# GpSimd's order in the differential attention written out, its casts and joins regrouped, and the retention's first scores one step later

## The chip, the cores and the metric

The kernel runs on one core of a Trainium2 chip. The metric is the device time of one execution in microseconds (us). The engines are TensorE (PE in the profile), VectorE (DVE), ScalarE (ACT), GpSimd (POOL) and SyncE (SP); SP only issues DMAs. GpSimd issues DMAs too, and those stand in its own instruction stream among its arithmetic.

## The reference, cut to what matters

The program is one layer of a diffusion backbone on 1024 tokens of width 1024, with 256 context tokens, batch 1, in float32. One input projection feeds two groups of four heads each: a two-way chunked retention, and a differential attention over 1280 keys. Their outputs side by side go through one output projection; a gated residual and a gated MLP with a convolution of width 3 follow.

```python
# retention, one chunk
scores = jnp.einsum('bhid,bhjd->bhij', qc, kc) * intra
o = (jnp.einsum('bhij,bhje->bhie', scores, vc)
     + jnp.einsum('bhid,bhde->bhie', qc * q_dec[..., None], S))
S = S * c_dec[:, None, None] + jnp.einsum('bhjd,bhje->bhde', kc * k_dec[..., None], vc)

# differential attention: q (B,H,2,Lq,d), k (B,H,2,Lk,d), v (B,H,Lk,dv)
s = jnp.einsum('bhmqd,bhmkd->bhmqk', qb, k).astype(jnp.float32) * scale
p = jax.nn.softmax(s, axis=-1)
a = p[:, :, 0] - lam * p[:, :, 1]
return jnp.einsum('bhqk,bhke->bhqe', a.astype(v.dtype), v)

# each head's output is scaled by its root mean square, then
out_lat = jnp.concatenate([y_ret_lat, y_diff_lat], axis=-1) @ w_out
x = x + g1 * y_lat
h2 = rms_norm(x, norm2_g[l]) * (1.0 + sc2) + sh2
x = x + g2 * conv_ffn(h2, w_up[l], conv_w[l], conv_b[l], w_down[l])
```

## The kernel before

Float32 operands of the projections are split into a high part and a low part (a cast and a subtraction), and each product is three matmuls, here called a triple. The stages lie one after the other on PE: modulation and projections of keys, values and gates; the projection of the queries, with the retention between its triples; the differential attention; the output projection; the MLP.

**Retention.** The projection calls `tick()` after each triple. `beside(outputs(), 1.35, -16.0)` sets a generator of retention steps beside it: its count starts at the third number and grows by the second at each triple, and each step that falls due is emitted there. The first step holds the first score matmuls, `pc<-st,rk`, whose operand `st` DVE makes by an addition (L466).

**Differential attention.** There are 32 units: four heads (h) by eight tiles of 128 queries (qt). A unit runs through the operations of `OPS` (`scores`, `least`, `exp`, `ratio`, ...). The loop over n is the software pipeline: in turn n, operation `op` is emitted for unit n - int(TAU[op]), in the order of the fractions of `TAU`. Turn n thus holds scores of unit n, `values` (pv, L972) of unit n - 3, and the norm of unit n - 4. For PE, DVE, ACT and SP `in_order` pins the engine's order to the order of emission (`FORCE`). GpSimd is not pinned: a scheduler places its instructions by its own model of time, and `tc.issue_after` only says behind which instruction one may come.

The names that the change touches:

- `ratio` (L951, L952): DVE's reciprocal and product for r; `combine` (L955): DVE's p0 += r * p1 over 1280 columns, from which PE transposes (pt, L960) and ACT copies back (aT, L966).
- `square`: ACT's sum of squares (jka, L981) and GpSimd's small product `e` (L983). `rstd`: DVE's `ssa` (L986), then GpSimd's power -0.5 (L987), called the root here. ACT's norm (L990) waits for the root, PE's `pty` (L995) for the norm, and DVE's low part (L1001) follows.
- `wo_gen`: twelve tiles of 128 x 512 for the output projection, four of the retention's output and eight of weights. GpSimd loads a tile into `woraw` (five buffers), ACT casts it (L1106, L1123), GpSimd subtracts for the low part (L1107, L1124).
- `joined_tokens`: for a head and a half of the queries GpSimd adds high and low part of the attention's output into a `woraw` buffer (L1130) and adds that by DMA onto sums in memory (L1132: t2 and t3, or t4). These sums are operands of the output projection, which multiplies sums and differences of blocks. They are `sgd_152` (t1) to `sgd_155` (t4) in the listings, and the sums of weights `wsd`.
- `load(n + 3)`: GpSimd issues the loads of later units' queries, keys and values (L1018, L1021, L1043).

At the attention's end SP issues the rows of x (L1228), the weight sums (L1100) and the operands `raw` (L1335, from t1, t2, ...) of the output projection. There DVE gates each output (L1351), adds it to x (L1352), and makes the low parts `wolo` (L1107) and `wlo` (L1197).

Of the kernel before, what the change touches and what calls it, by code (L numbers as in the profile page):

```python
# [17 lines left out]
P = 128  # L18
# [8 lines left out]
H = 4  # L27
# [39 lines left out]
FORCE = (mybir.EngineType.PE, mybir.EngineType.DVE, mybir.EngineType.Activation, mybir.EngineType.SP)  # L67


def r32(ap):  # L70
    return ap.bitcast(F32)
# [3 lines left out]
def kernel(  # L75
# [16 lines left out]
    nc = tc.nc  # L92
# [28 lines left out]
    def in_order(start, engines=FORCE):  # L121
        last = {}
        for ins in nc.cur_bb.bb.instructions[start:]:
            if ins.engine not in engines:
                continue
            if ins.engine in last:
                order_only(ins, last[ins.engine])
            last[ins.engine] = ins
# [12 lines left out]
    row_d = [dr.tile([32, 32], F32, name=f"row{i}") for i in range(4)]  # L141
# [7 lines left out]
    yr_d = dr.tile([P, H, 512], F32, name="yrd")  # L149
    sg_d = [dr.tile([P, H, 512], F32, name=f"sgd{i}") for i in range(4)]  # L150
    t1_d, t2_d, t3_d, t4_d = sg_d
    ws_d = [dr.tile([P, 4, 512], F32, name=f"wsd{i}") for i in range(4)]
    A11, A12, A21, A22 = [w_out[i][:, c : c + 4, :] for i in range(2) for c in (0, 4)]
# [7 lines left out]
    with ExitStack() as p1:  # L161
# [207 lines left out]
        def outputs():  # L369
            n_pairs, per_head = H * NT // 2, NT // 2  # L370
            pairs, more = {}, states((2, 3))
            for n in range(-2, n_pairs + 3):
                if n + 2 < n_pairs:
                    pairs[n + 2] = Pair(n + 2)
                if n == -2:
                    continue
                if n + 1 < n_pairs:
                    pairs[n + 1].score()
                forming = per_head <= n < 3 * per_head
                if n == per_head - 1 or forming and n % 2 == 0:  # L380
                    next(more)
                yield
                if 0 <= n < n_pairs:
                    pairs[n].output(0)
                yield
                if forming:
                    next(more)
                yield
                if n == n_pairs + 2:
                    for _ in range(4):  # L390
                        yield
                    pairs[n - 3].turn(newest[0])
                elif n >= 3:
                    pairs[n - 3].turn()
                if 0 <= n < n_pairs:
                    pairs[n].output(1)
                    pairs[n].squares()
                yield
                if 0 <= n - 1 < n_pairs:
                    pairs[n - 1].gate()  # L400
                    for _ in range({1: 2, 2: 2}.get(n, 0)):
                        weight_sum(last_y[0])
                if forming:
                    next(more)
                yield
                yield
# [9 lines left out]
        def beside(g, rate, due=0.0):  # L416
            for _ in side["g"]:
                pass
            side.update(g=g, rate=rate, due=due)
# [127 lines left out]
        with ExitStack() as p0:  # L547
# [151 lines left out]
            for k in range(KD):  # L699
# [28 lines left out]
                n = k + 4  # L728
# [179 lines left out]
        for made_key in keyed[:2]:  # L908
            order_only(made_key.ins, rk_turned.ins)
        wg = stream_block(0)  # L910
        beside(outputs(), 1.35, -16.0)
        transposed(wg, None, rtab, 64, 1.0, 0, by_head)
        rtab = load_rope(1)
        wg = stream_block(4)
# [176 lines left out]

    g1 = wo.tile([P, D], F32, name="g1")

    def out_weights(srcs, sl, eng=nc.sync, low=nc.vector, lag=0, after=(), free=0):
        raws = []
        srcs = [src[:, k, :] for src in srcs for k in range(4)]
        for k in range(len(srcs) + lag):
            if k < len(srcs):
                raw = wo.tile([P, 512], F32, name="woraw", bufs=5)
                wo_loads.append(eng.dma_start(out=raw, in_=srcs[k]))  # L1100
                raws.append(raw)
            yield
            if k >= lag:
                whi = wo.tile([P, 512], F32R, name="wohi", bufs=8)
                wlo = wo.tile([P, 512], F32R, name="wolo", bufs=8)
                wo_casts.append(nc.scalar.copy(whi, raws[k - lag]))  # L1106
                part = low.tensor_tensor(out=wlo, in0=raws[k - lag], in1=r32(whi), op=ALU.subtract)  # L1107
                for ins in after if k - lag >= free else ():
                    order_only(part.ins, ins.ins)
                sl.append((whi, wlo))  # L1110

    wo_first, wo_casts, wo_loads = [], [], []
    wo_gen = out_weights((A11, ws_d[0]), wo_first, nc.gpsimd, nc.gpsimd, 2)

    def first_tokens():
        raws = []
        for h in range(H + 2):
            if h < H:
                raws.append(wo.tile([P, 512], F32, name="woraw", bufs=5))
                nc.gpsimd.dma_start(out=raws[h], in_=yr_d[:, h, :])  # L1120
            yield
            if h > 1:
                nc.scalar.copy(yT[0][1][:, h - 2, :], raws[h - 2])  # L1123
                nc.gpsimd.tensor_tensor(out=yT[1][1][:, h - 2, :], in0=raws[h - 2], in1=r32(yT[0][1][:, h - 2, :]), op=ALU.subtract)  # L1124

    wo_gen = itertools.chain(first_tokens(), wo_gen)

    def joined_tokens(h, half):
        raw = wo.tile([P, 512], F32, name="woraw", bufs=5)
        nc.gpsimd.tensor_tensor(out=raw, in0=r32(yT[0][half][:, H + h, :]), in1=r32(yT[1][half][:, H + h, :]), op=ALU.add)  # L1130
        for to in (t4_d,) if half else (t2_d, t3_d):
            nc.gpsimd.dma_start(out=to[:, h, :], in_=raw, accum_op=ALU.add)  # L1132

    with ExitStack() as p2:
        at = p2.enter_context(tc.tile_pool(name="at", bufs=2, reuse_waits="tile"))
        psa = p2.enter_context(tc.tile_pool(name="psa", bufs=1, space=PSUM, reuse_waits="tile"))

        turns = {}
        start = len(nc.cur_bb.bb.instructions)
        order = sorted(TAU.items(), key=lambda it: it[1] % 1.0)  # L1140
        for n in range(n_units + 8):
            if 2 < n < n_units:
                units[n] = Unit(n)
                vars(units[n]).update(fore[n])
            if n == 9:
                with tc.issue_after(units[n - 5].pool_ins.ins):
                    nc.gpsimd.dma_start(out=g1, in_=row_d[0].rearrange("p c -> (p c)").partition_broadcast(P))
            if n in (6, 9, 15, 17, 21, 28):
                with tc.issue_after(units[n - 5].pool_ins.ins):
                    if n == 6:  # L1150
                        nc.gpsimd.dma_start(out=t1_d[:, H - 1, :], in_=yr_d[:, H - 1, :], accum_op=ALU.add)
                    elif n == 9:
                        nc.gpsimd.dma_start(out=t2_d[:, :, :], in_=t1_d[:, :, :])
                    else:
                        i, j, k = {15: (1, 0, 0), 17: (1, 0, 2), 21: (3, 1, 0), 28: (3, 1, 2)}[n]
                        nc.gpsimd.dma_start(out=ws_d[i][:, k : k + 2, :], in_=ws_d[j][:, k : k + 2, :], accum_op=ALU.add)
            if n in (14, 21, 29):
                nc.sync.dma_start(out=t4_d[:, (14, 21, 29).index(n), :], in_=t2_d[:, (14, 21, 29).index(n), :])
            for half, when in ((0, (12, 18, 26, 33)), (1, (16, 24, 31))):
                if n in when:  # L1160
                    with tc.issue_after(units[min(n - 5, n_units - 1)].pool_ins.ins):
                        joined_tokens(when.index(n), half)
            for op, t in order:
                u = n - int(t)
                if 0 <= u < n_units and (u > 1 or op not in EARLY) and (op, u) not in MOVED:
                    turns[op, u] = len(nc.cur_bb.bb.instructions)
                    units[u].run(op)
                    turns[op, u] = nc.cur_bb.bb.instructions[turns[op, u]]
                for o, v in MOVED.get((op, u), ()):
                    units[v].run(o)  # L1170
                if op == "f" and n >= 9 and n not in (12, 16, 18, 24, 26, 31, 33):
                    with tc.issue_after(units[min(n - 6, n_units - 1)].pool_ins.ins):
                        next(wo_gen, None)
            if n + 3 < n_units:
                after = units[n - 5].pool_ins if n >= 5 else last_va[0]
                with tc.issue_after(after.ins):
                    fore.append(load(n + 3))
        in_order(start)
    aload.close()


# [753 lines left out]
```

## Time and profile before

| what | value |
|---|---|
| median of 3 runs | 1365.8 us (1365.76 to 1365.85) |
| the profiled execution | 1365.33 us, span 1363.5 us, granted clock 0.998 |
| PE | 1348.6 us busy, 99% of the span |
| DVE, ACT, POOL | 998.3, 749.6 and 341.7 us busy |
| attention, 440 to 625.7 us | PE busy 183.6 of 185.7 us, POOL 91.5 |
| chain that ended last | PE 87%, DVE 5%, ACT 3%, issue 2%, DMA 1%, POOL 1% |

Times inside the profile count from the start of the span. A timeline row gives start, duration, engine, source line, operation, output and inputs, the number of instructions that the row joins, and in brackets the engine's idle time before it with what ended it. PE's matmuls are pipelined and their ends modelled: a row's duration may overlap the next row, so PE's progress is read from start to start.

### The profile page before, as it was taken

How to read it: one execution, taken by the hardware profiler on the slowest of the kernel's cores; microseconds unless marked ns; L12 is line 12 of the kernel's file. 1: busy time of each engine (PE TensorE's matmuls, PEld its weight loads, DVE VectorE, ACT ScalarE, POOL GpSimd, SP SyncE). 2: the span in 40 equal slices, each digit the busy share in tenths (PEclk: the TensorE clock that was granted, in tenths of full speed). 3: DMA queues.
4: the chain of work that ended last, by engine and by line, in shares of the span. 5: the costliest groups of instructions: out<-in, count | busy, mean ns of one | idle time of the engine just before them, and what ended most of it. 6: DMA issues, size and time to landing. Idle time of an engine off the chain costs nothing.

```text
span 1363.5 us, 19850 instructions
## 1 busy us (share of the span) xinstructions
PE 1348.6 (99%) x6978; PEld 1134.9 (83%) x6978; DVE 998.3 (73%) x1514; ACT 749.6 (55%) x1429; POOL 341.7 (25%) x433
## 2 busy tenths in 40 slices
PE   9999999999999999999999999999999999999997
PEld 6788888888898899998887788888888888888886
DVE  4746874425775899897989986677776777798856
ACT  4643312424765789997547555445554455455543
POOL 1210004403776436543021222221222110000001
PEclk9999999999999999999999999999999999999999
DMA  9567897655866769855954898988888875963523
GB/s 369 216 255 241 296 314 245 190 181 157 214 174 168 177 153 182 169 109 157 342 166 113 194 233 217 224 218 226 214 213 214 220 193 172 371 214 101 177 93 124
DMA packets 130492, 279.71 MB, mean 205 GB/s; under 512 B 13700, under 2 KB 34948, under 8 KB 129480
## 3 DMA queue, kind: packets, MB, share of 16 engines
q1 hardware_dynamic: 100440, 212.99, 45.8%
q0 software_dynamic: 29376, 64.00, 25.6%
q10 hardware_dynamic: 576, 1.44, 0.3%
q8 instruction: 55, 0.90, 0.3%
q14 instruction: 45, 0.37, 0.1%
HBM read 212.31 MB, written 69.75 MB: 207 GB/s over the span
## 4 chain that ended last, share of the span: by engine, by line
PE 87%; DVE 5%; ACT 3%; issue 2%; DMA 1%; POOL 1%; POOLq 0%; DVEq 0%; ACTq 0%
PE chain L135 6%; PE chain L133 6%; PE chain L134 6%; PE c L134 5%; PE c L133 5%; PE c L135 5%; PE pv L972 4%; PE pl L133 4%; PE pl L135 4%; PE pl L134 4%; PE pA L940 4%; PE pn L135 3%; PE pn L134 3%; PE pn L133 3%; PE third L134 3%; PE third L133 3%
## 5 line engine op out<-in xcount | busy, mean ns | idle before, releaser
L1269 POOL DMA_DIRECT2D cmb<-w_up x80 | 73.9, 1151 | 180.4 <-DMA cmb<-w_up 142.8
L133 PE MATMUL pl<-hT,whi 128*128 128x512 f32 x256 | 105.4, 412 | 0.0
L133 PE MATMUL chain<-T,whi 128*128 128x512 f32 x264 | 102.9, 391 | 0.0
L134 PE MATMUL chain<-T,whi 128*128 128x512 f32 x264 | 102.6, 389 | 0.0
L135 PE MATMUL chain<-T,wlo 128*128 128x512 f32 x264 | 102.4, 390 | 0.2 <-DVE wlo L1197 0.2
L135 PE MATMUL pl<-hT,wlo 128*128 128x512 f32 x256 | 100.1, 391 | 0.0
L134 PE MATMUL pl<-hT,whi 128*128 128x512 f32 x256 | 99.9, 390 | 0.0
L943 DVE TENSOR_REDUCE mt<-pA 128x1 f32<-128x1280 f32 x64 | 95.2, 1489 | 6.1 <-PE pA L940 4.6
L947 ACT ACTIVATE p<-pA,mt 128x1280 f32<-128x1280 f32 x64 | 85.5, 1336 | 9.4 <-DVE mt L943 8.7
L133 PE MATMUL c<-whi,ghl 128*128 128x512 f32 x232 | 90.2, 389 | 0.0
L134 PE MATMUL c<-wlo,ghl 128*128 128x512 f32 x232 | 90.2, 389 | 0.0
L135 PE MATMUL c<-whi,ghl 128*128 128x512 f32 x232 | 90.2, 389 | 0.0
L940 PE MATMUL pA<-ks,qhl 128*128 128x512 f32 (+1 forms) x384 | 89.6, 368 | 0.6 <-ACT p L947 0.5
L1193 ACT CAST whi<-cmb 128x512 fp32r<-128x512 f32 x60 | 37.5, 627 | 85.2 <-PE chain L134 63.0
L940 PEld LDWEIGHTS pA<-ks,qhl 128*128 128x128 f32 x384 | 68.1, 189 | 12.9 <-ACT p L947 1.3
L972 PE MATMUL pv<-va,aT 128*128 128x128 f32 x640 | 77.3, 276 | 0.8 <-DVE yT L1001 0.5
L972 PEld LDWEIGHTS pv<-va,aT 128*128 128x128 f32 x640 | 74.0, 192 | 2.3 <-DVE yT L1001 1.3
L1193 ACT CAST whi<-wra 128x512 fp32r<-128x512 f32 x54 | 33.1, 623 | 68.9 <-PE third L134 40.2
L133 PE MATMUL third<-yT,whi 128*128 128x512 f32 x168 | 65.4, 389 | 0.0
L134 PE MATMUL third<-yT,whi 128*128 128x512 f32 x168 | 65.4, 389 | 0.0
L135 PE MATMUL third<-yT,wlo 128*128 128x512 f32 x168 | 65.4, 389 | 0.0
L133 PE MATMUL pn<-whi,hT 128*128 128x512 f32 x160 | 64.7, 405 | 0.0
(342 smaller groups left out, 3842.2 us busy)
## 6 DMA issues: line engine op xcount, KB each, us to landing
cmb<-w_up POOLq DMA_DIRECT2D x80, 256.0 KB, 6.5
wm<-w_mod SPq DMA_DIRECT2D x32, 512.0 KB, 5.5
cmb<-w_up SPq DMA_DIRECT2D x60, 256.0 KB, 5.2
raw<-w_in SPq DMA_DIRECT2D x27, 512.0 KB, 5.7
wra<-w_up SPq DMA_DIRECT2D x23, 512.0 KB, 6.2
W<-w_down SPq DMA_DIRECT2D x44, 256.0 KB, 6.2
wrb<-w_up SPq DMA_DIRECT2D x40, 256.0 KB, 4.5
ad<-s SPq DMA_DIRECT2D x20, 512.0 KB, 5.7
```

Source lines behind the costliest of these rows:

```text
L133: mm(ps, lh, rh, start=first, stop=False, skip_group_check=more)
L134: mm(ps, lh, rl, start=False, stop=False, skip_group_check=more)
L135: return mm(ps, ll, rh, start=False, stop=last, skip_group_check=more)
L940: mm(self.pa[m][:, c0:c1], self.q[:, m, i, qs], self.k[:, m, c0:c1], start=(i == 0), stop=(i == 1))
L943: nc.vector.tensor_reduce(out=self.mt[:, m : m + 1], in_=self.pa[m][:, :LK], axis=AX.X, op=ALU.min)
L947: nc.scalar.activation(self.p[m], self.pa[m][:, :LK], AF.Exp, scale=-1.0, bias=self.mt[:, m : m + 1], accum_out=self.s[:, m : m + 1])
L972: mm(self.pv, self.aT[:, c, :], self.v[:, c, :], start=(c == 0), stop=(c == NKT - 1))
L1193: cast = nc.scalar.copy(hi, src)
L1269: nc.gpsimd.dma_start(out=o, in_=src, accum_op=ALU.add)
```

## The change

Four things are changed.

1. GpSimd's order in the attention is pinned as the other engines' is (`FORCE` plus `Pool`). In each turn it is: root, then at most one addition (a low part or a join), then DMA issues, then `e`, then the next units' loads. `beside_roots(n)` is called right behind `rstd` and holds all that was spread over three places.
2. A tile of `wo_gen` is loaded in one turn, cast by ACT two turns later, and its low part made by GpSimd one turn after the cast. Before, cast and low part were of one turn. No tile is taken in turns 13 and 21, nor where a join stands.
3. Joins have tiles of their own (`joined`, two buffers, in the pool `at`) and no longer take `woraw` buffers.
4. `beside(outputs(), 1.35, -17.6)`: the count starts 1.6 lower.

The diff, cut to its core:

```diff
-        beside(outputs(), 1.35, -16.0)
+        beside(outputs(), 1.35, -17.6)
...
-    wo_gen = out_weights((A11, ws_d[0]), wo_first, nc.gpsimd, nc.gpsimd, 2)
...
+    def out_ahead():
+        srcs = [yr_d[:, h, :] for h in range(H)] + [w[:, k, :] for w in (A11, ws_d[0]) for k in range(4)]
+        raws, parts = [], []
+        for n in range(len(srcs) + 3):
+            if n > 2:
+                hi, lo = parts[n - 3]
+                nc.gpsimd.tensor_tensor(out=lo, in0=raws[n - 3], in1=r32(hi), op=ALU.subtract)
+            if n < len(srcs):
                 raws.append(wo.tile([P, 512], F32, name="woraw", bufs=5))
-                nc.gpsimd.dma_start(out=raws[h], in_=yr_d[:, h, :])
+                nc.gpsimd.dma_start(out=raws[n], in_=srcs[n])
+            if 1 < n < len(srcs) + 2:
+                i = n - 2
...
+                cast = nc.scalar.copy(parts[i][0], raws[i])
...
             yield
...
     def joined_tokens(h, half):
-        raw = wo.tile([P, 512], F32, name="woraw", bufs=5)
+        raw = at.tile([P, 512], F32, name="joined", bufs=2)
...
+    def beside_roots(n):
+        for half, when in ((0, (12, 18, 26, 33)), (1, (16, 24, 31))):
+            if n in when:
+                joined_tokens(when.index(n), half)
+                break
+        else:
+            if n >= 9 and n not in (13, 21):
+                next(wo_gen, None)
+        if n == 6:
+            nc.gpsimd.dma_start(out=t1_d[:, H - 1, :], in_=yr_d[:, H - 1, :], accum_op=ALU.add)
+        elif n == 8:
+            nc.gpsimd.dma_start(out=g1, in_=row_d[0].rearrange("p c -> (p c)").partition_broadcast(P))
+        elif n == 9:
+            nc.gpsimd.dma_start(out=t2_d[:, :, :], in_=t1_d[:, :, :])
+        elif n in (15, 17, 22, 28):
+            i, j, k = {15: (1, 0, 0), 17: (1, 0, 2), 22: (3, 1, 0), 28: (3, 1, 2)}[n]
+            nc.gpsimd.dma_start(out=ws_d[i][:, k : k + 2, :], in_=ws_d[j][:, k : k + 2, :], accum_op=ALU.add)
...
-            for half, when in ((0, (12, 18, 26, 33)), (1, (16, 24, 31))):
-                if n in when:
-                    with tc.issue_after(units[min(n - 5, n_units - 1)].pool_ins.ins):
-                        joined_tokens(when.index(n), half)
...
-                if op == "f" and n >= 9 and n not in (12, 16, 18, 24, 26, 31, 33):
-                    with tc.issue_after(units[min(n - 6, n_units - 1)].pool_ins.ins):
-                        next(wo_gen, None)
+                if op == "f" and u >= 0:
+                    beside_roots(n)
...
-        in_order(start)
+        in_order(start, FORCE + (mybir.EngineType.Pool,))
```

In the change's file the lines of `wo_gen` and the joins have other numbers (subtraction L1119, load L1122, cast L1130, join L1139 and its DMA L1141, the rest L1152 to L1159), and all from the output projection on stand ten lower (L1228 is L1238 there).

GpSimd in the middle of the attention, from one root (L987) on, before:

```order
L987 TENSOR_TENSOR ssa<-ssa,mhalf 128x1
L1124 TENSOR_TENSOR yT_4484<-woraw,yT_4482 128x512
L1130 TENSOR_TENSOR woraw<-yT_4481,yT_4483 128x512
L983 TENSOR_TENSOR e<-sa 128x1
L1100 DMA woraw<-w_out 128x512
L1132 DMA sgd_153<-woraw 128x512
L1132 DMA sgd_154<-woraw 128x512
L987 TENSOR_TENSOR ssa<-ssa,mhalf 128x1
```

and now:

```order
L987 TENSOR_TENSOR ssa<-ssa,mhalf 128x1
L1139 TENSOR_TENSOR joined<-yT_4481,yT_4483 128x512
L1141 DMA sgd_153<-joined 128x512
L1141 DMA sgd_154<-joined 128x512
L983 TENSOR_TENSOR e<-sa 128x1
L987 TENSOR_TENSOR ssa<-ssa,mhalf 128x1
L1119 TENSOR_TENSOR yT_4484<-woraw,yT_4482 128x512
L1122 DMA woraw<-w_out 128x512
L983 TENSOR_TENSOR e<-sa 128x1
```

Two additions between two roots have become one behind each root, and `e` stands behind the DMA issues.

GpSimd at the attention's end, where the last join of t2 and t3 stands, before:

```order
L987 TENSOR_TENSOR ssa<-ssa,mhalf 128x1
L983 TENSOR_TENSOR e<-sa 128x1
L1130 TENSOR_TENSOR woraw<-yT_4481,yT_4483 128x512
L1132 DMA sgd_153<-woraw 128x512
L1132 DMA sgd_154<-woraw 128x512
L987 TENSOR_TENSOR ssa<-ssa,mhalf 128x1
L983 TENSOR_TENSOR e<-sa 128x1
L987 TENSOR_TENSOR ssa<-ssa,mhalf 128x1 x2
```

and now:

```order
L987 TENSOR_TENSOR ssa<-ssa,mhalf 128x1
L983 TENSOR_TENSOR e<-sa 128x1
L987 TENSOR_TENSOR ssa<-ssa,mhalf 128x1
L1139 TENSOR_TENSOR joined<-yT_4481,yT_4483 128x512
L1141 DMA sgd_153<-joined 128x512
L1141 DMA sgd_154<-joined 128x512
L983 TENSOR_TENSOR e<-sa 128x1
L987 TENSOR_TENSOR ssa<-ssa,mhalf 128x1
L983 TENSOR_TENSOR e<-sa 128x1
L987 TENSOR_TENSOR ssa<-ssa,mhalf 128x1
```

The join and its DMAs stand one root later: three roots followed them, and now two.

SP's queue at the same place (`x_4` to `x_7` are rows of x, `sgd_152` is t1 and `sgd_153` is t2), as a difference:

```order
-L1228 DMA x_7_6792<-x 128x1024
-L1335 DMA raw_6793<-sgd_152 128x2048
-L1100 DMA woraw<-wsd_159 128x512
-L1228 DMA x_4_6789<-x 128x1024
-L1228 DMA x_5_6790<-x 128x1024
-L1228 DMA x_6_6791<-x 128x1024
-L1100 DMA woraw<-wsd_159 128x512 x3
-L1335 DMA raw_6793<-sgd_153 128x2048
```

```order
+L1100 DMA woraw<-wsd_159 128x512 x4
+L1100 DMA woraw<-wsd_157 128x512
+L1238 DMA x_7_6792<-x 128x1024
+L1345 DMA raw_6793<-sgd_152 128x2048
+L1345 DMA raw_6793<-sgd_153 128x2048
+L1238 DMA x_4_6789<-x 128x1024
+L1238 DMA x_5_6790<-x 128x1024
+L1238 DMA x_6_6791<-x 128x1024
```

The weight sums have moved ahead, and the load of t2 now stands ahead of `x_4` to `x_6`.

More of the change, by code (lines that the diff above doesn't have):

```diff
@@ L1092, with out_weights @@
     g1 = wo.tile([P, D], F32, name="g1")
-    def out_weights(srcs, sl, eng=nc.sync, low=nc.vector, lag=0, after=(), free=0):
+    def out_weights(srcs, sl, lag=0, after=(), free=0):
         raws = []
@@ L1099, in out_weights @@
                 raw = wo.tile([P, 512], F32, name="woraw", bufs=5)
-                wo_loads.append(eng.dma_start(out=raw, in_=srcs[k]))
+                wo_loads.append(nc.sync.dma_start(out=raw, in_=srcs[k]))
                 raws.append(raw)
@@ L1106, in out_weights @@
                 wo_casts.append(nc.scalar.copy(whi, raws[k - lag]))
-                part = low.tensor_tensor(out=wlo, in0=raws[k - lag], in1=r32(whi), op=ALU.subtract)
+                part = nc.vector.tensor_tensor(out=wlo, in0=raws[k - lag], in1=r32(whi), op=ALU.subtract)
                 for ins in after if k - lag >= free else ():
@@ L1112 @@
     wo_first, wo_casts, wo_loads = [], [], []
-    wo_gen = out_weights((A11, ws_d[0]), wo_first, nc.gpsimd, nc.gpsimd, 2)
[L1115 to L1118, printed above, removed]
-                raws.append(wo.tile([P, 512], F32, name="woraw", bufs=5))
-                nc.gpsimd.dma_start(out=raws[h], in_=yr_d[:, h, :])
+    def out_ahead():
[6 more added lines that the diff above has]
+            if n < len(srcs):
+                raws.append(wo.tile([P, 512], F32, name="woraw", bufs=5))
+                nc.gpsimd.dma_start(out=raws[n], in_=srcs[n])
+            if 1 < n < len(srcs) + 2:
+                i = n - 2
+                if i < H:
+                    parts.append(tuple(yT[a][1][:, i, :] for a in range(2)))
+                else:
+                    parts.append(tuple(wo.tile([P, 512], F32R, name=nm, bufs=8) for nm in ("wohi", "wolo")))
+                    wo_first.append(parts[i])
+                cast = nc.scalar.copy(parts[i][0], raws[i])
+                if i >= H:
+                    wo_casts.append(cast)
             yield
[L1122 to L1126, printed above, removed]
+    wo_gen = out_ahead()
     def joined_tokens(h, half):
-        raw = wo.tile([P, 512], F32, name="woraw", bufs=5)
+        raw = at.tile([P, 512], F32, name="joined", bufs=2)
         nc.gpsimd.tensor_tensor(out=raw, in0=r32(yT[0][half][:, H + h, :]), in1=r32(yT[1][half][:, H + h, :]), op=ALU.add)
@@ L1132, in joined_tokens @@
             nc.gpsimd.dma_start(out=to[:, h, :], in_=raw, accum_op=ALU.add)
+    def beside_roots(n):
[3 more added lines that the diff above has]
+                break
+        else:
+            if n >= 9 and n not in (13, 21):
[9 more added lines that the diff above has]
+            nc.gpsimd.dma_start(out=ws_d[i][:, k : k + 2, :], in_=ws_d[j][:, k : k + 2, :], accum_op=ALU.add)
     with ExitStack() as p2:
@@ L1144 @@
                 vars(units[n]).update(fore[n])
[L1145 to L1156, printed above, removed]
             if n in (14, 21, 29):
                 nc.sync.dma_start(out=t4_d[:, (14, 21, 29).index(n), :], in_=t2_d[:, (14, 21, 29).index(n), :])
-            for half, when in ((0, (12, 18, 26, 33)), (1, (16, 24, 31))):
-                if n in when:
-                    with tc.issue_after(units[min(n - 5, n_units - 1)].pool_ins.ins):
-                        joined_tokens(when.index(n), half)
             for op, t in order:
```

## The prediction

> **What bounds the kernel now.** The page's head comes first:
>
> ```profile
> span 1363.5 us, 19850 instructions
> PE 1348.6 (99%) x6978; PEld 1134.9 (83%) x6978; DVE 998.3 (73%) x1514; ACT 749.6 (55%) x1429; POOL 341.7 (25%) x433
> ```
>
> PE is busy nearly throughout, so only its pauses can be won: 15 us, and what hides in busy times because its matmul ends are modelled. The waits of PE around the attention name the places:
>
> ```profile
> PE pc L269 <- DVE st L466: 0.4, 1, 0.4
> PE pv L972 <- DVE yT L1001: 0.5, 2, 0.2
> ```
>
> The 0.5 us understates the second. A unit's `values` (pv) come once a step, so the starts of pv in PE's timeline measure steps:
>
> ```profile
> 513.02 2.40 PE L972 MATMUL pv<-va,aT 128*128 128x128 f32 x20
> 518.77 2.40 PE L972 MATMUL pv<-va,aT 128*128 128x128 f32 x20
> 524.72 0.50 PE L972 MATMUL pv<-va,aT 128*128 128x128 f32 x3
> ...
> 625.70 0.49 PE L972 MATMUL pv<-va,aT 128*128 128x128 f32 x2
> L972 PE MATMUL pv<-va,aT 128*128 128x128 f32 x380 | 45.8, 276 | 0.5 <-DVE yT L1001 0.5
> ```
>
> (The last row groups the same stretch: 380 records, 20 to a step, are 19 steps.) A clean step is 518.77 - 513.02 = 5.75 us. Nineteen would be 109.25; they took 625.70 - 513.02 = 112.68. So **3.43 us** are lost between GpSimd, DVE and ACT in these steps. Next, the timelines of DVE and of POOL show how:
>
> ```profile
> 526.15 0.22 DVE L952 SCALAR_TENSOR_TENSOR r<-r,sa,nlam 128x1 f32<-128x1 f32 x1
> ...
> 531.98 1.59 DVE L952 SCALAR_TENSOR_TENSOR r<-r,sa,nlam 128x1 f32<-128x1 f32 x1 [0.18 <-ACT p L947]
> ```
>
> ```profile
> 526.48 1.53 POOL L983 TENSOR_TENSOR e<-sa 128x1 f32<-128x1 f32 x1
> ...
> 531.91 1.64 POOL L1124 TENSOR_TENSOR yT<-woraw,yT 128x512 fp32r<-128x512 f32 x1
> ...
> 590.05 0.19 POOL L983 TENSOR_TENSOR e<-sa 128x1 f32<-128x1 f32 x1
> ```
>
> r on one column takes 0.22 us, but 1.59 where GpSimd began a large addition 0.07 us earlier: it ended with that addition. The other way, `e` takes 0.19, but 1.53 beside the combine. Four such r rows appear (531.98, and near 544, 579, 621). That they reach PE is read in the chain that ended last, at the fourth:
>
> ```profile
> 621.11 1.23 DVE r L952
> ...
> 625.70 2.50 PE pv L972 x20
> ```
>
> **The change, part by part.**
>
> *One addition behind each root.* The addition that met r was a second one, behind a first and the issues. Now each follows its root directly. What lies there is seen at a root that an addition follows already (POOL, then DVE):
>
> ```profile
> 588.27 0.55 POOL L987 TENSOR_TENSOR ssa<-ssa,mhalf 128x1 f32<-128x1 f32 x1 [3.10 <-DVE ssa L986]
> 588.80 1.28 POOL L1130 TENSOR_TENSOR woraw<-yT,yT 128x512 f32<-128x512 f32 x1
> ...
> 590.38 0.96 POOL L1132 DMA_DIRECT2D sgd<-woraw  x1
> ...
> 592.27 1.22 POOL L1132 DMA_DIRECT2D sgd<-woraw  x1
> ```
>
> ```profile
> 589.50 0.34 DVE L1001 SCALAR_TENSOR_TENSOR yT<-pty,subg,yT 128x128 fp32r<-128x128 f32 x1
> 589.76 1.49 DVE L943 TENSOR_REDUCE mt<-pA 128x1 f32<-128x1280 f32 x1
> ...
> 592.85 1.55 DVE L955 SCALAR_TENSOR_TENSOR p<-p,r,p 128x1280 f32<-128x1280 f32 x1
> ```
>
> The addition ran 588.80 to 590.08 beside the low part and the start of a reduction (1.49 us as everywhere), and none is longer for it; r is due only after the second reduction, at 591.2. So additions meet no r. By the step starts the lost time has two parts: that at the clashes, and that at ACT's casts, which the change keeps. ACT's timeline has a cast and, in a step without one, ACT's free time:
>
> ```profile
> 523.76 0.62 ACT L1123 CAST yT<-woraw 128x512 fp32r<-128x512 f32 x1
> 494.25 0.59 ACT L966 COPY aT<-pt 128x512 f32<-128x512 f32 x1 [0.59 <-PE pt L960]
> ```
>
> A castless step leaves ACT 0.59 us free, one cast takes 0.62, and the step 518.77 to 524.72 took 5.95: 0.20 more. In runs of neighbouring cast steps I count this loss at every second one. By the order, ACT's casts now fall in pipeline turns 11, 14, 15, 17, 19, 20, 22, 23, 25 and 27 to 29, with four such pairs: 4 x 0.20 = 0.80 us stay. I keep 0.2 more for `e` or loads late at a step. The attention is thus worth 3.43 - 0.80 - 0.2 = **2.4 us**. Bounds: 3.3 if the spread casts fit into ACT's free time, 1.0 if half the clash time returns at other places (below).
>
> `e` behind two issues meets the combine: 588.27 + 0.55 + 1.28 + 0.96 + 1.22 = 592.28, the combine at 592.85. It then ends with the combine, still 1 us ahead of the next root, and nothing stands behind it but unit loads in every fourth turn. Only turn 17 has an addition, two issues, `e` and loads: 0.2 us there, within what I kept.
>
> [...]
>
> *Joins in buffers of their own.* They end one wait, a weight load behind a join's DMA (POOL's timeline):
>
> ```profile
> 582.60 0.59 POOL L1100 DMA_DIRECT2D woraw<-wsd  x1 [2.15 <-DMA sgd<-woraw]
> ```
>
> The root stood behind it and was late; that loss is already within the 3.43. The loads of g1 (a turn earlier) and of one weight sum (a turn later) are issued before 590 and read behind 620 only: nothing.
>
> *The retention's scores.* A start lower by 1.6 at 1.35 a triple is 1.2 triples; the order shows one triple between:
>
> ```profile
> 321.42 0.39 PE L135 MATMUL pl<-hT,wlo 128*128 128x512 f32 x1
> 322.22 0.71 PE L269 MATMUL pc<-st,rk 128*128 128x128 f32 x4 [0.41 <-DVE st L466]
> ...
> 323.00 0.39 PE L134 MATMUL pl<-hT,whi 128*128 128x512 f32 x1
> 323.23 0.40 PE L135 MATMUL pl<-hT,wlo 128*128 128x512 f32 x1
> 321.47 0.69 DVE L466 TENSOR_TENSOR st<-st,xb 128x512 f32<-128x512 f32 x1
> ```
>
> Matmuls start 0.23 us apart (323.00 to 323.23), pc started 0.80 behind its forerunner: 0.57 lost. A triple is 0.68 and covers it: st is done at 322.16, pc due at 322.33. Gain **0.57 us**; bounds 0.7 (a small wait later goes as well) and a loss of 0.3 (a later step, now on other DVE neighbours, waits instead).
>
> *The end of the attention.* Here the change costs. The last join and its DMAs move behind the next root (POOL, then SP, two landing times each from a window of its own, and the rate of all queues in 40 slices of 626 to 655):
>
> ```profile
> 633.62 1.80 POOL L1132 DMA_DIRECT2D sgd<-woraw  x2 [0.90 <-POOL woraw L1130]
> 635.15 0.86 POOL L987 TENSOR_TENSOR ssa<-ssa,mhalf 128x1 f32<-128x1 f32 x1
> ```
>
> ```profile
> 636.19 1.39 SPq L1228 DMA_DIRECT2D x<-x  x3
> sgd<-woraw POOLq DMA_DIRECT2D x1, 256.0 KB, 4.6
> raw<-sgd SPq DMA_DIRECT2D x1, 1024.0 KB, 4.8
> GB/s 0 0 0 0 0 0 113 215 452 418 359 252 68 65 178 138 99 153 164 234 373 404 412 415 398 393 424 444 463 412 396 407 418 407 435 424 407 429 441 356
> ```
>
> Before, the DMAs were issued at 633.62 and 634.2, ahead of the root at 635.15. Now the join of 1.28 us (588.80) starts behind that root, at about 635.7, and ends at 637.0; its first DMA, issued at 637.3, lands 4.6 us later, at 641.9. SP's load of t2 waits for it, and `x_4` to `x_6`, issued from 636.19 until now, stand behind it: from about 642.4. The 1 MB of t2 lands 4.8 us after its issue at 642.0, at 646.8; then each row of 0.5 MB takes 1.25 us at the 420 GB/s of the later slices, with a start 0.4 later: 648.4, 649.7 and 650.9. DVE adds each row in its pinned order, ahead of the `wolo` rows:
>
> ```profile
> 650.37 1.29 DVE L1107 TENSOR_TENSOR wolo<-woraw,wohi 128x512 fp32r<-128x512 f32 x2 [0.56 <-DMA wra<-w_up]
> 662.43 1.28 DVE L1351 TENSOR_TENSOR gated<-o,g 128x512 f32<-128x512 f32 x2
> 663.14 0.62 PE L133 MATMUL o<-wohi,yT 128*128 128x512 f32 x2
> ```
>
> `x_6` added at 651.0 to 651.7 lets the wolo rows start some 1.4 us later than 650.37. From there to the gating at 662.43 DVE has no gap, so that comes 1.4 late too. PE takes the banks that it frees at 663.37 and 664.05 (the second of the x2, and three matmuls later), and the gatings end at 663.1 and 663.7: a margin of about 0.3. PE then waits 1.4 - 0.3 = **1.1 us**. Bounds: 0, if the weight sums, out of the way earlier, let x land 1.2 sooner; 2.4, if the load of t2 and the three rows share the queue and all land last, near 652.
>
> *Sum.* 1365.33 - 0.57 - 2.4 + 1.1 = 1363.5 for the profiled execution. The median of the runs stands 0.47 above the profiled time, so the median is **1363.9 us**, 1.9 us or 0.14% less.
>
> **The rivals.**
>
> *The end costs nothing.* x lands in time, since `wsd` loads no longer share the queue (they moved far ahead). Against it: three rows of x behind a load that waits for a later join. Then, with 2.4 to 3.3 from the attention, 1365.8 - 0.57 - 2.4 = 1362.8 down to 1361.9.
>
> *The clash time returns elsewhere, and the end costs its full price.* Most of 3.43 stays, through r blocked by slipped additions or through ACT, and the attention gives 1.0: 1365.8 - 0.57 - 1.0 + 1.1 to 2.4 = 1365.3 to 1366.6, no change to be seen. For it: neighbouring cast steps stay, and one addition late by 1.1 us is enough; against it: the clean rows at 588.80 and 589.76.
>
> *Slower: the pinned order makes roots queue.* In the free order GpSimd let nothing stand long ahead of a root. Pinned, an addition that waits for ACT's cast, or a load for a buffer, holds `e`, the loads and the next root; the wait at 582.60 was 2.15 us. Then ACT's norm, pty, DVE's low part and pv follow late. It decides once GpSimd's work in a turn exceeds the 5.75 us step, or a wait in it some 1.5 us. If three of the turns with two issues lose 1.5 each and the end its 2.4: 1365.8 - 0.57 + 4.5 + 2.4 - 2.4 = 1369.7. Against it: casts lie a whole step ahead, and POOL's longest new row of work in a turn, 592.28 - 588.27 = 4.0 us, is within the step.
>
> **How the numbers follow.** Forecast 0.48 (1363.0 to 1365.0), first rival 0.26, second 0.19, slower 0.07. A difference below 0.2%, 2.7 us, is about what a measurement of this kernel can't tell from no change. Below 1363.07 lie the first rival and a little of the forecast: 0.31; above 1368.5 the last: 0.06; between 0.63. The range, 1361.9 to 1366.6, takes in the first two rivals.
>
> **What would show it.** Right: r at 0.22 in all steps of 513 to 625; pv starts 5.75 apart except 5.95 at cast pairs; pc without a wait near 322; the first DVE x addition of the output projection waiting near 645 to 648 for DMA, and PE waiting once about 1 us for `gated` near 661. Wrong: r rows of 1.2 or more, roots with late starts, or a gated row in time with x on hand.

## The result: 0.6% slower, and the profile after

| | before | after |
|---|---|---|
| median of 6 runs each | 1365.79 us (1365.45 to 1367.01) | 1373.73 us (1373.02 to 1375.51) |
| ratio, with its 95% interval | | 1.0059 (1.0046 to 1.0072) |
| span of the profiled execution | 1363.5 us | 1371.4 us |

The change costs 8 us where 1.9 us less were forecast; the time lies outside the range. The head of the page of the changed kernel, and then the three largest of its waits of PE over the whole span (us in total, times, longest):

```profile
span 1371.4 us, 19845 instructions
PE 1351.1 (99%) x6978; PEld 1135.5 (83%) x6978; DVE 995.8 (73%) x1514; ACT 749.5 (55%) x1429; POOL 341.5 (25%) x433
```

```profile
PE o L133 <- DVE gated L1361: 2.2, 2, 2.0
PE po L277 <- ACT yr L307: 1.6, 1, 1.6
PE pu L349 <- ACT o L282: 1.4, 1, 1.4
```

Both waits that the change aimed at are gone (`pc` for `st` at 322, `pv` for `yT`). New ones stand in the retention (the rows for po and pu among them), and one of 2.0 us behind the attention. Where the time went is read from PE's starts. Its first `pA` row and two rows of pv, from windows of PE's timeline of the changed kernel:

```profile
447.43 1.30 PE L940 MATMUL pA<-ks,qhl 128*128 128x512 f32 x6
518.57 2.40 PE L972 MATMUL pv<-va,aT 128*128 128x128 f32 x20
629.45 2.40 PE L972 MATMUL pv<-va,aT 128*128 128x128 f32 x20
```

and the first of these before (the other two are the rows at 513.02 and 625.70 of the prediction):

```profile
442.33 1.30 PE L940 MATMUL pA<-ks,qhl 128*128 128x512 f32 x6
```

| place | before | after | later by | gained or lost up to there |
|---|---|---|---|---|
| start of the attention | 442.33 | 447.43 | 5.10 | 5.1 lost in the stages before, the retention among them |
| pv, step 1 | 513.02 | 518.57 | 5.55 | 0.45 lost |
| pv, step 20 | 625.70 | 629.45 | 3.75 | **1.80 gained** in 19 steps |
| end of the span | 1363.5 | 1371.4 | 7.9 | **4.15 lost** behind the attention |

**The attention** does what the prediction said of it. The r rows of its 19 steps and the next, by a view of the line L952 (shortest, middle and longest duration in ns), where the longest was 1.59 us before:

```profile
L952 DVE SCALAR_TENSOR_TENSOR r<-r,sa,nlam x20: 218/220/220, 514.1 to 625.1; 128x1 f32<-128x1 f32 x20
```

No r is held by an addition any more. What stays is ACT's casts: pv rows of PE's timeline, and the cast between the first two (ACT).

```profile
524.33 2.40 PE L972 MATMUL pv<-va,aT 128*128 128x128 f32 x20
530.09 2.40 PE L972 MATMUL pv<-va,aT 128*128 128x128 f32 x20
536.02 2.41 PE L972 MATMUL pv<-va,aT 128*128 128x128 f32 x20
```

```profile
529.32 0.63 ACT L1130 CAST yT<-woraw 128x512 fp32r<-128x512 f32 x1
```

The step from 524.33 took 5.76, clean. The next, behind the cast at 529.32, took 5.93. So the first cast of a pair already costs nearly its 0.2; the second, at 535.08, costs 0.12, and the single one at 546.88 makes its step 5.94.

**The retention** now waits for loads. ACT's waits from 310 to 445, the row for the states' keys, after and before:

```profile
ACT ks L333 <- DMA kvs<-kvg: 11.9, 7, 5.2
```

```profile
ACT ks L333 <- DMA kvs<-kvg: 2.4, 4, 0.8
```

The longest of them, and what stood behind it on ACT; then PE, whose state product `pu` waits:

```profile
369.41 0.51 ACT L333 ACTIVATE ks<-kvs,kd 128x256 f32<-128x256 f32 x1 [5.19 <-DMA kvs<-kvg]
...
371.58 0.59 ACT L282 COPY o<-po 128x512 f32<-128x512 f32 x1
```

```profile
372.22 0.49 PE L349 MATMUL pu<-kvs,ks 128*128 128x128 f32 x2 [1.39 <-ACT o L282]
```

The copy of `po` (three other rows lie between), which frees the bank that PE takes next, stands behind that `ks` in ACT's order and so came behind a load: 371.58, after the wait of 5.19. Why the load was late, SP's queue shows, after and then before (`kvo` holds the values of an output pair, `kvs` the keys and values of a state step):

```profile
359.61 0.38 SPq L242 DMA_DIRECT2D kvs<-kvg  x1
...
365.96 0.32 SPq L242 DMA_DIRECT2D kvo<-kvg  x1
366.37 0.38 SPq L242 DMA_DIRECT2D kvs<-kvg  x1
```

```profile
360.22 0.32 SPq L242 DMA_DIRECT2D kvs<-kvg  x1
364.43 0.32 SPq L242 DMA_DIRECT2D kvo<-kvg  x1
```

Before, the last kvs load ahead of the kvo load goes at 360.22. After, one kvs load fewer goes ahead: the next stands behind a kvo load that waits until 365.96 for its buffer, which GpSimd's `y` frees (POOL), and it is the one for which ACT waits:

```profile
365.19 0.74 POOL L296 TENSOR_TENSOR y<-y,kvo 128x256 f32<-128x256 f32 x1
```

The scheduler, which sets SP's order here, exchanged pairs of kvs and kvo loads when all output steps moved a triple.

**Behind the attention** the chain of the prediction holds step by step until the load of t2. POOL, then SP, then the two issues with their size and time to landing, each from a window of its own:

```profile
639.29 1.28 POOL L1139 TENSOR_TENSOR joined<-yT,yT 128x512 f32<-128x512 f32 x1
641.48 1.79 POOL L1141 DMA_DIRECT2D sgd<-joined  x2 [0.90 <-POOL joined L1139]
```

```profile
645.51 0.32 SPq L1345 DMA_DIRECT2D raw<-sgd  x1
645.94 1.50 SPq L1238 DMA_DIRECT2D x<-x  x3
raw<-sgd SPq DMA_DIRECT2D x1, 1024.0 KB, 6.9
x<-x SPq DMA_DIRECT2D x3, 512.0 KB, 8.9
```

DVE's rows at that place, and PE's:

```profile
653.73 0.69 DVE L1362 TENSOR_TENSOR x<-x,gated 128x512 f32<-128x512 f32 x1 [5.64 <-DMA x<-x]
...
657.13 1.29 DVE L1107 TENSOR_TENSOR wolo<-woraw,wohi 128x512 fp32r<-128x512 f32 x2
...
666.76 1.28 DVE L1361 TENSOR_TENSOR gated<-o,g 128x512 f32<-128x512 f32 x2
```

```profile
665.23 0.39 PE L135 MATMUL o<-wohi,yT 128*128 128x512 f32 x1
667.58 0.47 PE L133 MATMUL o<-wohi,yT 128*128 128x512 f32 x1 [1.96 <-DVE gated L1361]
...
669.06 0.63 PE L133 MATMUL o<-wohi,yT 128*128 128x512 f32 x1
669.89 0.79 PE L133 MATMUL o<-wohi,yT 128*128 128x512 f32 x1 [0.20 <-DVE gated L1361]
```

With matmuls 0.23 apart, the pause 665.23 to 667.58 costs 2.12 us, and 669.06 to 669.89 another 0.60. From 668.97 on PE ran at half its clock: the table of windows (window and its length, busy time of PE, PEld, DVE, ACT and POOL with their counts, then the granted clock, DMA share and GB/s):

```profile
668.97:672.39 3.42, 3.22 (x8) 2.04 (x8) 3.42 (x7) 2.19 (x4) 0.00 (x0) 0.50 0.42 173
```

From 669.89 to a full rate at 672.51 six intervals took 2.62 us instead of 1.38: 1.24 more. The three sum to 3.96 of the 4.15 (the second pause lies in the stretch of half clock, so a part of its 0.60 is the clock's too).

### The profile page after: what moved, and what is told of

The parts are those of the page before. It is cut to its first block, busy times and chain, and to the rows that moved or that the text cites. A ratio compares the mean times of both kernels' runs of the same rounds, so it can differ in the third digit from the quotient of the medians.

```text
span 1371.4 us, 19845 instructions
## 1 busy us (share of the span) xinstructions
PE 1351.1 (99%) x6978; PEld 1135.5 (83%) x6978; DVE 995.8 (73%) x1514; ACT 749.5 (55%) x1429; POOL 341.5 (25%) x433
## 4 chain that ended last, share of the span: by engine, by line
PE 84%; DVE 5%; issue 3%; POOL 3%; ACT 3%; DMA 2%; SPq 0%; POOLq 0%; ACTq 0%; DVEq 0%
PE chain L135 6%; PE chain L133 6%; PE chain L134 6%; PE c L134 5%; PE c L133 5%; PE c L135 5%; PE pA L940 5%; PE pv L972 5%; PE pl L135 3%; PE pl L133 3%; PE pl L134 3%; PE pn L135 3%; PE pn L134 3%; PE pn L133 3%; PE third L133 3%
```

## The experiments

The theories, named by a letter where the expectations do so. **S**: the later scores alone cost the retention its time. **J**: the last join, a root later, costs the end its time. **E**: what costs the end is not the join; a row of x is held by two things, the load of t2 ahead of it on SP and the last `e`, pinned behind a root, which frees the buffer that the row waits for. **K**: the retention's loss is the order of kvo and kvs loads on SP. **Q**: the order of the load of t2 and the rows of x on SP costs the end, however early the join is.

### The two edits apart

The later scores alone, in the kernel before:

```diff
-        beside(outputs(), 1.35, -16.0)
+        beside(outputs(), 1.35, -17.6)
```

> The kernel before with the retention's count started 1.6 lower, and nothing else. Theory S (this edit alone loses the time before the attention, by loads that come late to ScalarE in the retention): about 1365.8 + 4.9 = 1370.7 us, the first pv of the attention near 466 us. Rival (the edit gains its 0.6 us as predicted, and the loss needs the other edits): 1365.2 us.

Measured: 1372.61 us, ratio 1.0044 (1.0029 to 1.0059), 6.5 us more (4.9 forecast) than the kernel before beside it (1366.15; some 1 us of it, by an estimate from its granted clock of 0.72 from 402 to 408 us, may be a lowered clock behind the longest pause, told of at the end). ACT's waits in the retention have the same row as after:

```profile
ACT ks L333 <- DMA kvs<-kvg: 13.6, 5, 4.9
```

Everything else, with the scores where they were (the line above, undone in the changed kernel):

> The changed kernel with the retention's count put back. Theory S: the 4.9 us before the attention go, what stays is 1.6 won in the attention and 4.1 lost behind it: about 1365.8 - 1.6 + 4.1 = 1368.3 us. Rival (the loss before the attention stays, since pinning or buffers cause it): about 1373 us.

Measured: 1368.42 us, 1.0015 (1.0006 to 1.0025). The two losses, 6.5 and 2.3 against 1366.15, sum to 8.8 for the 8.0 of the whole. In the profiled execution the attention starts at 442.45, as before (442.33), so the 5.1 us up to there are the later scores'. S is shown: the smallest edit, forecast as a gain, is the largest loss.

The rest is not composed in this run's profiled execution as in the change. Its two largest waits of PE:

```profile
PE o L133 <- ACT wohi L1106: 2.5, 1, 2.5
PE pA L940 <- DMA ks<-dk: 1.5, 1, 1.5
```

The first is again behind the late rows of x: loads of weight sums wait on SP until 654.72 for buffers that DVE's `wolo` frees late. The second is in the attention, whose 19 steps took 112.50 us instead of the change's 110.88. The pinned order issues the loads of later units' queries, keys and values together; of the loads issued from 505 to 532 us, those of the keys landed 7.1 us after issue before (median of two), 12.9 in the change and 14.8 here. Of the seven traces with the pinned order only this one has the wait, so it is a risk of that order; why the loads took longer here is open.

The first retention step alone a triple later, the rest where it was:

```diff
+        def first_later():
+            for i, _ in enumerate(outputs()):
+                if i == 0:
+                    side["due"] += 1.6
+                yield
+
-        beside(outputs(), 1.35, -16.0)
+        beside(first_later(), 1.35, -17.6)
```

> The kernel before, with only the first step of the retention a triple later; the count gets its 1.6 back behind that step, so all later steps fall where they fell. Theory S (the loss comes from the later steps being late, the first score's wait is covered by a triple): 1365.8 - 0.6 = 1365.2 us, no wait at the first pc, ScalarE waits for kvs as little as before (2.4 us). Rival (delaying the first scores alone sets off the chain): near 1371 us.

Measured: 1365.30 us, 0.9997 (0.9988 to 1.0007), against 1365.97 beside it. PE has no wait for `st` any more and ACT's wait for kvs is 1.4 us in all. The 0.7 us has the predicted size, but isn't told from none. The predicted gain, if it is there, belongs to the first step; the loss belongs to the steps behind it, which moved as well.

### The retention: whose order

In the kernel with the later scores alone, the kvo loads issued by GpSimd instead of SP, so that they can't hold a kvs load:

```diff
-            nc.sync.dma_start(out=kv, in_=kvg_d[g][:, h, s0 : s0 + 2])
+            (nc.gpsimd if nm == "kvo" else nc.sync).dma_start(out=kv, in_=kvg_d[g][:, h, s0 : s0 + 2])
```

> The kernel before with the retention's count 1.6 lower, and the loads of values and gates (kvo) issued by GpSimd, so that the loads of kvs no longer stand behind them in SP's queue. Theory K (SP's queue: kvo waits there for GpSimd's y, and kvs, which ScalarE waits for, stands behind): ScalarE's wait for kvs falls from 12 us to 3 or less, and most of the 5 to 6 us come back: 1366 us. Rival (the steps are late by themselves, as VectorE and ScalarE have another order): near 1371 us, with waits of PE on ScalarE left. GpSimd issues 16 DMAs more, about 0.9 us each, so up to 1 us may be lost to it.

Measured: 1375.94 us, 1.0075 (1.006 to 1.009). ACT's wait for kvs shrank to 1.0 us, as wanted, but the time didn't come back. PE's waits in the retention are others:

```profile
PE pyt L301 <- DVE S L357: 2.8, 2, 1.8
PE po L277 <- DVE S L357: 1.4, 1, 1.4
PE pc L269 <- DVE S L357: 1.4, 1, 1.4
```

GpSimd's issues stand among its products: from 310 to 445 us 13 of these loads took 9.3 us of it, 0.72 each, and the edit adds this work to the engine on which `y` and the roots `ss` wait. It doesn't decide about K.

The same aim on SP: each kvo load is put behind the next kvs load (`order_only(a, b)` places a behind b on its engine).

```diff
-            nc.sync.dma_start(out=kv, in_=kvg_d[g][:, h, s0 : s0 + 2])
+            loaded = nc.sync.dma_start(out=kv, in_=kvg_d[g][:, h, s0 : s0 + 2])
+            if nm == "kvo":
+                pending.append(loaded)
+            else:
+                while pending:
+                    order_only(pending.pop().ins, loaded.ins)
...
```

> The kernel before with the retention's count 1.6 lower, and SP issues each load of values (kvo) behind the next load of keys (kvs), so that kvs doesn't stand behind the wait of kvo for GpSimd's y. The queue keeps its issuing engine, unlike the run with the loads by GpSimd. Theory K (the two loads have changed places in SP's queue): ScalarE's wait for kvs falls from 13.6 us to 5 or less, and most of the 5 to 6 us come back: 1365.2 to 1367 us. Rival (a triple later, the ring of PE, VectorE, GpSimd and loads is too long by itself): 1370 us or more, and the wait moves to another place.

Measured: 1368.41 us, 1.0015 (1.0006 to 1.0024): of the 6.5 us some 4.2 are back, against 1366.09 beside it; 1365.2 to 1367 was forecast, and ACT's wait for kvs fell to 7.3 us, not to 5 or less. In the profiled executions the attention starts at 444.46 here and at 449.13 with the later scores alone (442.33 before); about 1.5 us of the 4.67 between them are, by an estimate from the same 0.72, the lowered clock told of at the end. K is shown for the rest of these 4.67. One pair was still in the other order, at 392.5, and ACT still waited 1.93 us for that kvs at 396; PE's pauses that were left lay right behind it, at 397 to 402. So that pair was exchanged too:

```diff
-                pending.append(loaded)
+                pending.append((h, 2 if (h, g) == (3, 1) else 1, loaded))
...
```

(the number says behind how many kvs loads the kvo load goes).

> The run with every kvo load behind the next kvs load (1368.4) and, for the first pair of the last head, behind the next two. All of the retention's loss there stood behind that one pair: kvo issued at 392.50 when GpSimd's y freed its buffer, kvs at 392.91 behind it, ACT's ks waiting 1.93 us for it at 396.01. If the order of the two loads on SP is the cause of that rest too, the wait at 396 goes, PE no longer waits at 397 to 402, and the time is 1365.3 to 1366.6, about the kernel before's 1366.0. If instead the scores that are one triple late (y at 392.5 instead of 389.7) cost it, or the state products, the wait moves to another operand of the same steps and the time stays within 1367.6 to 1369.0. A time in between would mean that kvo, now behind a second load, is itself late for po.

Measured: 1368.97 us, 1.0025 (1.0015 to 1.0034), no better. ACT's wait at 396 is gone, and PE's waits there are the same to the tenth (1.1 for `sc`, 0.5 for `S`), as is the start of the attention, 444.43. So K fell for what is left. DVE's rows there (L302 is the gating of the retention's output, L280 the scores' product with the decay), and PE's:

```profile
401.53 0.35 DVE L302 SCALAR_TENSOR_TENSOR o<-o,ss,gn 128x128 f32<-128x128 f32 x1 [2.00 <-POOL ss L297]
401.80 0.69 DVE L280 TENSOR_TENSOR sc<-pc,dec 128x512 f32<-128x512 f32 x1
```

```profile
402.54 0.71 PE L278 MATMUL pc<-st,rk 128*128 128x128 f32 x4 [1.11 <-DVE sc L280]
```

The product that frees the bank of `pc` stands behind a gating row that waits 2.00 us for GpSimd's root of a step a triple late. That this is what is left of the loss, 2.1 us by the start of the attention, is argued from the rows and has not been tried.

### The end of the attention: which of three

All these have the scores at -16.0, and the first four also place the load of t3 behind a row of x. First the join as early as before:

```diff
-        for half, when in ((0, (12, 18, 26, 33)), (1, (16, 24, 31))):
+        for half, when in ((0, (12, 18, 26)), (1, (16, 24, 31))):
...
+                if op == "l" and n == 32:
+                    joined_tokens(3, 0)
...
```

> As the last one, and the last join of t2 and t3 put a root earlier, behind the low part of the last unit that it reads. Theory J (the late join delays the load of t2, and the rows of x queued behind it): the loss behind the attention goes, about 1364.2 us, no wait of PE for gated. Rival Q (it is the order of SP's queue, the load of t2 ahead of three rows of x, that costs, however early the join is): rows of x still land late by the 1 MB, some 2.5 us, and about 1.5 us stay: 1365.7 us.

Measured: 1368.95 us, 1.002 (1.001 to 1.003). J fell; Q foresaw that a loss stays, but 1.5 us of it. A wait in another place took over (PE), and DVE and SP show why:

```profile
PE pty L995 <- ACT oa L990: 2.5, 1, 2.5
```

```profile
646.43 0.69 DVE L1366 TENSOR_TENSOR x<-x,gated 128x512 f32<-128x512 f32 x1 [4.92 <-DMA x<-x]
```

```profile
637.66 0.32 SPq L1347 DMA_DIRECT2D raw<-sgd  x1
641.14 1.28 SPq L1240 DMA_DIRECT2D x<-x  x3
```

Here x comes behind t2 and also 3.5 us after it: the first row of x waited until 641.14 for the buffer that GpSimd's last `e` frees. In the pinned order that `e` (640.92) stands behind a root (640.41) that waited 3.88 us for DVE. On DVE x stands ahead of the last unit's `ssa`, so the root, ACT's norm and PE's `pty` follow late. That is DVE's order in the kernel before too (x at 642.49, `ssa` at 643.86); in the change `ssa` (647.55) stands ahead of x (653.73). So the late x costs PE at `pty` here and at gated there: DVE's order, which no edit named, moved as well.

Then the rows of x ahead of the load of t2 on SP, the join late as in the change:

```diff
-        nc.sync.dma_start(out=raw[:, :n, :], in_=src[:, :n, :])
+        operand = nc.sync.dma_start(out=raw[:, :n, :], in_=src[:, :n, :])
+        if src is t2_d:
+            order_only(operand.ins, x1_loads[6].ins)
+            for t in range(4):
+                order_only(x1_loads[t].ins, operand.ins)
+        elif src is t3_d:
+            order_only(operand.ins, x1_loads[3].ins)
```

> The changed kernel with the retention's count put back, the last join as late as in the change, but SP issues x_4 to x_6 and three loads of weights ahead of the load of t2. Theory J and Q both: the rows land some 7 us earlier, and the wait at gated goes, 1364.2 us. If instead the late operand t2 itself is what the end waits for: VectorE waits at the parts made from it, and 2 us or more stay: 1366 us or more.

Measured: 1368.36 us, 1.0021 (1.0011 to 1.003). The rows of x went ahead, but only at 639.58, when that `e` (639.37) had run, and DVE waited 4.92 us for them. J and Q, which both foresaw 1364.2, fell. That t2 itself is late would fit the number, but x is what DVE waits for, and a run below has t2 late without a loss. Then the early join with the `e` of the last two units a root earlier:

```diff
+                if (op, n) in (("Q", 32), ("f", 33)):
+                    units[n - 2].floor()
```

(`floor()` emits `e`, which `square` emits otherwise.)

> The changed kernel without the retention's edit, the last join a root earlier, and the products e of the last two units made right behind the e and the root that free their buffers, so that x_4 no longer waits for an e behind the last root but one. Theory E (x_4 is held by two things, the load of t2 ahead of it and the pinned e): x_4 is issued near 638 instead of 641 us, lands near 644, VectorE's wait there is about 1 to 2 us instead of 4.9, PE waits 0 to 1 us: 1364.5 to 1365.3 us. Rival (only SP's order counts): no better than the run with the early join alone, 2 to 3 us above before.

Measured: 1368.54 us, 1.0019 (1.001 to 1.0028), no better, as the rival said. The rows of x are free at 636.3, earlier than the 638 of the forecast, but stand behind the load of t2, issued at 635.87 and landed 7.5 us later; the first row is added at 644.71, and DVE waits 4.84 us for it where 1 to 2 were forecast. Freeing the buffer alone is thus not enough. Both together, the join late again:

> The changed kernel without the retention's edit, x_4 to x_6 issued ahead of the load of t2, and the products e of the last two units early; the last join stays late. Theory E: x_4 is issued near 636.5 us as in the kernel before, and the loss behind the attention goes: 1364.2 us. Rival J (the late join itself costs, through t2): t2 lands near 652, VectorE's parts of it are due at 657, so at most 1 us: 1365.2 us.

Measured: **1364.25 us**, 0.9990 (0.9981 to 0.9999), against 1365.97. SP and DVE:

```profile
633.98 1.29 SPq L1244 DMA_DIRECT2D x<-x  x3
642.30 0.33 SPq L1351 DMA_DIRECT2D raw<-sgd  x1
```

```profile
639.31 0.69 DVE L1374 TENSOR_TENSOR x<-x,gated 128x512 f32<-128x512 f32 x1
```

The join is as late as in the change, t2 is loaded at 642.30, and nothing waits for it: PE's longest pause there is 0.2 us. So the late join costs nothing by itself. The loss takes either of two things, x behind t2's load in SP's order or x's buffer held by a pinned `e`; each alone is enough, and removing one leaves it. E is shown in this form.

Whose doing is SP's order? In the kernel before, only the joins' own buffers:

```diff
-        raw = wo.tile([P, 512], F32, name="woraw", bufs=5)
+        raw = at.tile([P, 512], F32, name="joined", bufs=2)
```

> The kernel before with buffers of their own for the joins, and nothing else; GpSimd's order stays with the scheduler. Theory P (the attention's gain comes from additions no longer meeting r, by the pinned order): r rows above 1 us stay, the late root near 583 us goes, 0.3 us won: 1365.5 us. Rival (the waits for buffers made the additions slip, so buffers alone win it): no r row above 1 us, the 19 steps from 513 us take 111 instead of 112.7 us, 1364.2 us.

Measured: 1369.97 us, 1.0029 (1.0017 to 1.0041), where both forecasts were below the kernel before. The clashes of r stay, as P said:

```profile
L952 DVE SCALAR_TENSOR_TENSOR r<-r,sa,nlam x20: 207/220/1593, 515.0 to 628.0; 128x1 f32<-128x1 f32 x20
```

and the loss at the end is there (PE waits 2.6 us for the norm), with SP's order as in the change:

```profile
638.53 0.32 SPq L1335 DMA_DIRECT2D raw<-sgd  x1
638.96 1.61 SPq L1228 DMA_DIRECT2D x<-x  x3
```

Here and in the change SP issues five loads of weight sums ahead of `x_4` (from 593 and 605 us on; before, one at 630.16 and the next behind it, at 637.69), for which the buffers that joins no longer take leave room; that the scheduler puts t2 ahead of x for this reason is argued, not shown. So the joins' buffers are enough for the end's loss without the pinned order, which in turn brings the attention's gain.

### A version that beats both

The change with the rows of x first, `e` early, and only the first retention step later:

> GpSimd's order pinned as in the change, x_4 to x_6 issued ahead of the load of t2, the products e of the last two units early, and only the first step of the retention a triple later. If the gains add: 1365.8 - 1.8 from the attention and its end, - 0.6 from the first scores: 1363.4 us. If not, as the run without the retention's part, 1364.2 us.

Measured: **1364.38 us**, 0.9988 (0.9979 to 0.9997), against 1366.09: 1.7 us less than the kernel before and 9.3 less than the change. It isn't told from the version without the later step (1364.25), so that the gains add is not shown.

## Why the prediction was wrong

**What bounds the kernel** was read rightly: the clashes of r and GpSimd's additions cost PE time in the attention, and the pinned order removed all of them.

**"One addition behind each root", 2.4 us: right in kind, too large.** Measured 1.80 (0.2 in the one execution where the keys came late). The steps kept 110.88 - 109.25 = 1.63 us of loss where 1.0 was kept. The mis-sized part is the cast: counted at every second cast of neighbouring steps, it costs 0.12 to 0.20 in nine steps, single ones too. ACT's 0.59 us free in a castless step was no cover for 0.62 of cast. That `e` beside the combine costs nothing was right: it took 1.6 us in three turns without a longer step.

**"The retention's scores", a gain of 0.57 with a loss of 0.3 at worst: the step that failed.** The runs showed a loss in its place: 5.1 us up to the attention's start in the change, 6.5 by this edit alone. The prediction costed the first step, whose wait went (none at 322; a gain of 0.7 us in the run of that step alone, not told from none). But the edit moves all output steps by a triple, and those it priced by "a later step, now on other DVE neighbours" only. It read PE's order around one place and left out SP's queue in the retention, where the change exchanges kvs and kvo loads; a kvs load then waits behind one whose buffer GpSimd frees, and ACT waits with it (11.9 us where it was 2.4), the rows behind its `ks` too. Undoing the exchange brought most of the loss back; the cause of the last 2.1 us stays open.

**"The end of the attention", 1.1 us, bounds 0 to 2.4: right in kind, too small.** Taking off the 3.75 us by which PE was late, the chain was: join at 635.54 (forecast 635.7), sum landed at 641.74 (641.9), t2's load issued at 641.76 (642.0). Then the load took 6.9 us instead of 4.8, with the rows of x behind it in the same queues; the last row landed at 652.4, the place named as the upper bound (near 652), where 650.9 was taken. The time of 4.8 came from the load of t1 at 629.61, with no such neighbours; t2's own load in the kernel before, issued at 640.14 among others, took 9.0. `wolo` was 3.0 later than PE instead of 1.4. The margin was about 0.9, not 0.3, since PE pauses at the bank that the earlier gating frees (660.01 before, 666.76 after). So 2.7 us of pauses, and on top 1.24 at the lowered clock, which stood nowhere in the sum.

**"Joins in buffers of their own", nothing: wrong.** The text took only weight loads into account; the edit alone is enough for SP to take t2's load ahead of x, and the time then rises by 3.9 us. The prediction did see that order, but laid its cost to the late join, which costs nothing if x goes first and its buffer is free.

**The rivals.** "Slower" had the right side and the wrong place: no root queued in the attention. Its price, 4.5 us there, wasn't paid; the larger part of the loss lay in a stage that no rival named. "The end costs nothing" and "the clash time returns" are both out: the end cost 4.15 us, and the attention gave 1.8, not 1.0. (The 1.1 us by which one addition must be late for the clash time to return is an estimate, r's due time less the end of an addition, 591.2 - 590.08.)

## What to carry to other kernels

A shift of a stage against its neighbours must be followed on every queue whose order a scheduler sets, the loads' queue above all: here one load that waited for its buffer until 365.96 held the loads behind it, and the engine that then waited 5.19 us held another in turn (PE, 1.39). Where a loss has two causes of which each is enough, undoing one shows nothing; only undoing both, and each apart, does. A landing time read from a transfer without neighbours is no price for one among others: the same 1 MB took 4.8 us without them, and with them 9.0 and 9.6 us in the kernel before, 6.9 and 9.8 in the change.

## What was not expected of the hardware

PE's granted clock fell behind short pauses in three executions. In the change a pause of 2.35 us from start to start (665.23 to 667.58) was followed from 668.97 on by 3.42 us at half the clock (0.50 in the row 668.97:672.39 above), which cost at least 1.24 us beside the 2.12 of the pause itself. Eight profiled executions have a pause of 2.2 to 3.0 us from start to start. Three show the fall: the change (2.35), the later scores alone (2.61) and the rows of x first (2.86). The windows of the last two, with a granted clock of 0.72, and that of the early join, where it stayed at 1.00:

```profile
402.00:408.00 6.00, 6.00 (x30) 5.17 (x29) 2.26 (x7) 3.41 (x14) 4.01 (x5) 0.72 0.80 217
```

```profile
646.00:652.00 6.00, 5.32 (x17) 4.25 (x18) 1.98 (x4) 0.77 (x2) 0.19 (x1) 0.72 1.03 427
```

```profile
646.00:652.00 6.00, 3.69 (x17) 3.06 (x18) 3.12 (x7) 0.88 (x3) 0.55 (x1) 1.00 1.01 365
```

Five of the eight don't show it, with pauses of 2.20 to 2.97, so the length alone doesn't settle it. What does is open: that the pause lowers the clock is read from the order of the two in three executions, and no run moved a pause or changed its length alone.
